# Expert weights of a layer's start in shorter runs and asked for earlier, with a longer search for addresses

## The chip, the core and the metric

The kernel runs on one core of a Trainium2 chip. The metric is the time of one execution on the device, in microseconds. TensorE (PE) multiplies matrices, VectorE (DVE), ScalarE (ACT) and GpSimd (POOL) do the work between, and SyncE (SP) issues transfers. Transfers from memory (HBM) into on-chip memory (SBUF) run on 16 DMA engines, which serve the queues of SP, ACT and POOL together. SBUF has 128 partitions; a transfer writes each partition's part as one or more contiguous runs.

## What is computed

Two layers over 512 latent tokens and 256 context tokens of width 1024, all in float32. Each layer mixes tokens in four branches, gates and merges them, multiplies by an output projection, adds the result to the residual, and then sends tokens through 16 experts chosen by the experts themselves. Cut to what matters here:

```python
x = x + gt1 * (merge(branches(h)) @ w_out)       # output projection and residual
h2 = modulate(rmsnorm(x), sh2, sc2)
aff = softmax(h2 @ w_router)                     # (tokens, 16)
g, idx = top_k(aff.T, 2 * N // 16)               # 64 of 512 latent, 32 of 256 context tokens each
xe = h2[idx]                                     # gathered rows
hid = silu(xe @ w_gate[e]) * (xe @ w_up[e])      # 1024 -> 1408
x = x + gt2 * scatter_add(idx, (hid @ w_down[e]) * g)
```

The last layer leaves the context tokens out after their keys and values. An expert's three matrices are 17.3 MB; all experts of both layers together are 554 MB.

## The kernel before

**Stages.** A layer is: projections, attention and gates (the mixers); `out_and_route`, which multiplies by the output projection in two halves of 512 columns, adds the residual, normalises, computes router affinities and the top-k, and stores the normalised rows `h` and intermediate `x_res` to buffers in HBM (`h2s`, for the context `h2c`) from which they can be gathered; `experts`, a loop over 16 experts. Layer 0 has three groups of gathered rows (two of latent tokens, one of context), layer 1 has two.

**Expert weights.** An expert has six blocks of 128 partitions by 5,632 floats (22,528 bytes a partition, 2.88 MB): two of gate and up weights for the first half of the contraction (A), two for the second (B), two of down weights (D). A block is one load with one run of 22,528 bytes per partition; a half block, one run of 11,264 bytes. All are issued on SP's queue by `ex_load` (lines 1403 for halves and 1397 for whole blocks) in the order of use. `queued` (from line 1380) keeps few in flight: a whole block's load waits until the load two before it has landed, a half's until the one two before a half; the first load after expert 0's gathers also waits for these gathers. SP issues in order, so whatever waits there holds what stands behind.

**The start of a layer's experts.** The first eight blocks are listed in `early` (line 1146): four halves of A and four of B of expert 0, then two whole blocks of expert 1's A and two of expert 0's D. `out_and_route` issues two of them behind the first residual, four after the loop of the second half of the projection; `tail`, called from `experts`, issues the rest (in layer 0 two are left until after the gathers). Eight whole blocks are as much as the arena holds.

**The arena.** Weights and the mixers' large tiles lie in one arena of 183,296 bytes per partition. The kernel is built twice: the first build gives each tile's life, from which `place` finds an address for each (first fit in order of birth, and a tile that finds none goes to the front of the order); the second build uses them. A tile that takes the place of an earlier one waits for that one's last reader.

**The stores and the gather.** `store_tokens` (line 1375) stores 128 rows as two DMAs of 64 rows of 4,096 bytes, on ACT's queue: per 128 latent tokens one pair to `xs` (in layer 1 to `out`), one to `h2s`. POOL's `gather` (line 1440) of expert 0 reads `h2s` by indices `idx` (line 1289), so it waits for all stores to `h2s`. DVE transposes the gathered rows to `xT` (line 1449), and PE multiplies (`gu_ps`, line 1467).

**Output projection weights.** `w_out` comes in six pieces of three or two row blocks, `wo_raws` (line 368, on SP), each cast by ACT and split by DVE into high and low parts (`wo_w`, lines 146 and 147). The gates' weights go the same way (`craw`, `cw`, 72 tiles). The residual's loads (`x_res`, lines 1367 and 1369) stand on SP's queue among them.

Of the kernel before, what the change touches and what calls it, by code (L numbers as in the profile page):

```python
# [19 lines left out]
D = 1024  # L20
# [3 lines left out]
L = 2  # L24
# [3 lines left out]
WB = 5632  # L28
QUEUED = 2
# [23 lines left out]
ARENA = 183296  # L53

# [12 lines left out]
def place(lives, room):  # L67


    order = sorted(range(len(lives)), key=lambda n: lives[n][0])  # L70
    for _ in range(1000):
        offs = {}
        for n in order:
            a, z, size = lives[n]
            near = [(offs[m], offs[m] + lives[m][2], *lives[m][:2]) for m in offs]
            busy = [(p, e) for p, e, f, t in near if f <= z and t >= a]
            best = None
            for o in sorted({0, room - size} | {e for _, e, _, _ in near} | {p - size for p, _, _, _ in near}):
                if o < 0 or o + size > room or any(o < e and p < o + size for p, e in busy):
                    continue  # L80
                key = max((t for p, e, f, t in near if t < a and p < o + size and o < e), default=-1), o
                if best is None or key < best:
                    best = key
            if best is None:
                break
            offs[n] = best[1]
        else:
            return [offs[n] for n in range(len(lives))]
        order.remove(n)
        order.insert(0, n)  # L90
    raise ValueError("no room")
# [6 lines left out]
class Block:  # L98
    def __init__(self, ctx, tc, io, out, plan=None):

        self.tc, self.nc, self.io, self.out, self.plan = tc, tc.nc, io, out, plan
        self.asked = []
# [334 lines left out]
    def stage1(self, l, extra=()):  # L437
        nc, io = self.nc, self.io
        last = l == L - 1
# [97 lines left out]
        self.proj("na", 0, lhs, qk, evac_qk(NA, ssn, 8, 64), fill=run([]), wait=6)  # L537
        self.proj("df", 1, lhs, qk, evac_qk(DF, ssd, 16, 32), fill=run(skewed(na_vec, na_tr)))
# [590 lines left out]
    def out_and_route(self, l, xs_src, x_dst, ctx_dst):  # L1129
        nc, io = self.nc, self.io  # L1130
        last = l == L - 1
# [15 lines left out]
        early += [lambda e=e, p=p: self.ex_load(l, e, p, 1) for e, p in ((1, "A"), (1, "A"), (0, "D"), (0, "D"))]  # L1147
# [164 lines left out]
        with self.tc.manual_schedule(engines=IN_ORDER):  # L1312
            stores = []
            resid(0, 0, acc.pop(order[0]))
            for _ in range(2):
                early.pop(0)()
# [28 lines left out]
            for _ in range(4):  # L1345
                early.pop(0)()
# [41 lines left out]
    def ex_load(self, l, e, part, n):  # L1388
# [3 lines left out]
        src = self.io["w_ex"][l, e]  # L1392
        b0 = 2 * "ABD".index(part)
        if n:
            t = self.Q([n, WB], "w_ex")
            at = b0 + (len(blocks) if part == "D" else len(blocks) // 2)
# [359 lines left out]
```

## Time and profile before

| | us |
| --- | --- |
| Median of three runs | 2761.74 (2754.11 to 2763.66) |
| Profiled execution, its own time | 2758.79 |
| Span of the profiled execution | 2756.7 |
| PE busy | 2423.7 (88%) |
| DVE, ACT, POOL busy | 991.1, 566.5, 454.9 |
| HBM read | 734 MB |

In the profile a row of the order of time gives start, length, engine, line, operation, `out<-in` and in brackets the idle time ahead of it with what ended it. SPq and ACTq are the queues on which SP and ACT issue transfers: a row there is the issue, not the transfer; rows in sequence are merged, with their count at the end, and the length then reaches from the first to the last. Tables by stretch give each engine's busy time within it, the granted TensorE clock as a share of full speed, the share of the DMA engines' time and what they moved.

### The profile page before, as it was taken

Reading aid. Unit: us, or ns where it says so; the run is one execution under the profiler, and the core shown is the slowest. Engines: PE = TensorE matmul, PEld = TensorE weight load, DVE = VectorE, ACT = ScalarE, POOL = GpSimd, SP = SyncE. Lnnn points to the kernel's source line nnn. Section 1 sums busy time; section 2 is a strip of 40 time slices with the busy share of each in tenths; the row PEclk is TensorE's granted clock in tenths of the full one; section 3 lists DMA queues with packets and bytes.
Section 4 is the critical chain, followed back from the end, with each engine's and each line's share of the span. In section 5 each row is a group of like instructions: output and inputs, shape, how many; then the busy total and the mean of one; then the engine's idle time right before and its main releaser. Section 6 shows DMA issues by size and latency. Waiting matters only on the chain. (4 is left out here: it accounts for less than half of the span.)

```text
span 2756.7 us, 48426 instructions
## 1 busy us (share of the span) xinstructions
PE 2423.7 (88%) x21318; PEld 1685.5 (61%) x21318; DVE 991.1 (36%) x1997; ACT 566.5 (21%) x1082; POOL 454.9 (17%) x335
## 2 busy tenths in 40 slices
PE   4889999999969999999998799999973977777776
PEld 3668988899844556777775577777861423222222
DVE  4975547553251111121112666477440110110100
ACT  4333334432310000000000434344320000000000
POOL 1532111121141111011101121011131110010100
PEclk9989999999979999999999899999986999999999
DMA  7574462431379999999998576544457999999998
GB/s 260 186 228 142 131 170 73 125 118 47 118 261 416 418 414 410 414 411 413 408 414 331 175 220 198 170 134 138 117 205 322 419 421 423 416 418 422 418 421 326
DMA packets 128177, 776.72 MB, mean 282 GB/s; under 512 B 13408, under 2 KB 51552, under 8 KB 101856
## 3 DMA queue, kind: packets, MB, share of 16 engines
q1 hardware_dynamic: 109888, 728.80, 67.8%
q0 software_dynamic: 11776, 25.44, 3.8%
q10 hardware_dynamic: 6304, 19.40, 2.4%
q8 instruction: 167, 2.74, 0.4%
q14 instruction: 42, 0.34, 0.0%
HBM read 734.01 MB, written 39.58 MB: 281 GB/s over the span
## 5 line engine op out<-in xcount | busy, mean ns | idle before, releaser
L1467 PE MATMUL gu_ps<-w_ex,xT 128*32 128x352 f32 x10240 | 819.4, 474 | 151.8 <-DMA w_ex<-in_w_ex 94.3
L1467 PEld LDWEIGHTS gu_ps<-w_ex,xT 128*32 128x32 f32 x10240 | 482.1, 113 | 484.3 <-issue 246.2
L577 PE MATMUL gate_ps<-hh,cw 128*128 128x384 f32 (+1 forms) x1536 | 451.8, 361 | 0.0
L1500 PE MATMUL dn_ps<-w_ex,hidT 128*32 128x512 f32 x2816 | 344.8, 596 | 38.3 <-DMA w_ex<-in_w_ex 36.4
L1476 ACT ACTIVATE hid<-gu_ps 128x352 f32<-128x352 f32 x80 | 37.1, 463 | 1290.4 <-PE gu_ps L1467 1290.4
L577 PEld LDWEIGHTS gate_ps<-hh,cw 128*128 128x128 f32 x1536 | 283.8, 190 | 27.9 <-issue 5.7
L577 PE MATMUL gate_ps<-hl,cw 128*128 128x384 f32 (+1 forms) x768 | 274.6, 358 | 0.0
L1500 PEld LDWEIGHTS dn_ps<-w_ex,hidT 128*32 128x32 f32 x2816 | 117.3, 110 | 231.9 <-issue 191.9
L1502 DVE SCALAR_TENSOR_TENSOR y_e<-dn_ps,gval,gt 128x512 f32<-128x512 f32 x32 | 24.0, 751 | 460.1 <-PE dn_ps L1500 460.1
L1477 DVE TENSOR_TENSOR hid<-hid,gu_ps 128x352 f32<-128x352 f32 x80 | 41.7, 521 | 363.8 <-ACT hid L1476 254.4
L577 PEld LDWEIGHTS gate_ps<-hl,cw 128*128 128x128 f32 x768 | 145.7, 190 | 9.1 <-issue 0.4
L147 DVE TENSOR_TENSOR cw<-craw,cw 128x1280 fp32r<-128x1280 f32 (+1 forms) x72 | 112.2, 1560 | 33.8 <-ACT cw L146 33.6
L991 POOL TENSOR_TENSOR acc<-acc,sg 128x384 f32<-128x384 f32 (+1 forms) x48 | 64.6, 1346 | 358.0 <-DVE sg L981 278.9
L1494 DVE SCALAR_TENSOR_TENSOR y_e<-dn_ps,gval,gt 128x256 f32<-128x256 f32 x16 | 7.7, 484 | 320.4 <-PE dn_ps L1492 320.4
L1481 POOL DMA_INDIRECT out<-y_e,idx x16 | 25.7, 1609 | 581.3 <-DVE y_e L1502 581.3
L1481 POOL DMA_INDIRECT cs<-y_e,idx x16 | 27.1, 1691 | 509.5 <-DVE y_e L1494 509.5
L255 DVE SCALAR_TENSOR_TENSOR ada_acc<-w_ada_k,scT,ada_acc 128x1024 f32<-128x1024 f32 x68 | 94.1, 1393 | 18.4 <-DMA w_ada_k<-in_w_ada 18.3
L1492 PE MATMUL dn_ps<-w_ex,hidT 128*32 128x256 f32 x1408 | 100.6, 379 | 0.0
L146 ACT CAST cw<-craw 128x1280 fp32r<-128x1280 f32 (+1 forms) x72 | 89.2, 1241 | 42.5 <-PE branch_ps L975 18.5
L971 ACT ACTIVATE sg<-gate_ps 128x384 f32<-128x384 f32 (+1 forms) x96 | 50.5, 526 | 187.3 <-PE gate_ps L577 175.1
L981 DVE SCALAR_TENSOR_TENSOR sg<-sg,branch_ps 128x384 f32<-128x384 f32 (+1 forms) x72 | 42.9, 596 | 112.6 <-PE branch_ps L975 105.3
L1492 PEld LDWEIGHTS dn_ps<-w_ex,hidT 128*32 128x32 f32 x1408 | 64.4, 110 | 22.9 <-issue 1.8
(342 smaller groups left out, 3194.6 us busy)
## 6 DMA issues: line engine op xcount, KB each, us to landing
w_ex<-in_w_ex SPq DMA_DIRECT2D x184, 2816.0 KB
w_ada_k<-in_w_ada SPq DMA_DIRECT2D x80, 512.0 KB
craw<-in_w_gb SPq DMA_DIRECT2D x64, 640.0 KB
w_ex<-in_w_ex SPq DMA_DIRECT2D x16, 1408.0 KB
qkv_raws<-in_w_qkv SPq DMA_DIRECT2D x12, 768.0 KB
w_ada<-in_w_ada SPq DMA_DIRECT2D x4, 1536.0 KB
wo_raws<-in_w_out SPq DMA_DIRECT2D x8, 768.0 KB
na_st<-qk_job SPq DMA_DIRECT2D x10, 512.0 KB
```

The lines of the kernel that those rows point to most:

```text
L146: self.nc.scalar.copy(hi, src)
L147: self.nc.vector.tensor_sub(lo, src, hi.bitcast(F32))
L255: nc.vector.scalar_tensor_tensor(a, t, sc, a, op0=OP.mult, op1=OP.add)
L577: nc.tensor.matmul(ps, w[:, lw, k], self.hT(lh, k, t0, t1), start=(k == 0 and s == 0), stop=(k == 7 and s == 2))
L971: nc.scalar.activation(sg, pg, AF.Tanh, scale=0.5)
L981: nc.vector.scalar_tensor_tensor(o, sg, 1.0, pb, op0=OP.add, op1=OP.mult)
L991: nc.gpsimd.tensor_add(ac, ac, sg)
L1467: nc.tensor.matmul(PG[e, g][s][32 * j:32 * j + 32], XT[e][:, g, c], self.w_gu(e, c, s, j), start=(c == 0), stop=(c == 7))
L1477: nc.vector.tensor_mul(t[:, g], t[:, g], pu)
L1481: nc.gpsimd.indirect_dma_start(out=x, out_offset=bass.IndirectOffsetOnAxis(ap=idx, axis=0), in_=y, in_offset=None, compute_op=OP.add)
L1492: nc.tensor.matmul(ps[32 * j:32 * j + 32], HT[e][:, 2, k], self.w_dn(e, k, 256 * j, 256 * j + 256), start=(k == 0), stop=(k == 10))
L1500: nc.tensor.matmul(ps[32 * q:32 * q + 32], HT[e][:, g, k], self.w_dn(e, k, 512 * h, 512 * h + 512), start=(k == 0), stop=(k == 10))
```

## The change

The first eight blocks of each layer lie in a new array `w_head` as 32 pieces of 128 by 1,408 floats, so that a whole block comes in four runs of 5,632 bytes per partition and a half in two; the destination in SBUF and the bytes are as before. `early` is issued earlier: right behind the residual's loads at the start of `out_and_route` two halves in layer 0 and five in layer 1, then two and one behind the first residual, four and two after the loop, the rest in `tail` as before. `place` is divided into three parts by two marks (the middle of layer 0's transition to the experts, and a point in layer 1's projections); within each it tries orders with a tile that found no room re-inserted at random, and lets whole and half blocks start at multiples of their size only.

```diff
+RUN = 1408
+HEAD = ((0, "A"), (0, "B"), (1, "A"), (0, "D"))
 QUEUED = 2
...
+SEEDS = 6, 1, 149
...
         early = [lambda p=p: self.ex_load(l, 0, p, 0) for p in "AAAABBBB"]
-        early += [lambda e=e, p=p: self.ex_load(l, e, p, 1) for e, p in ((1, "A"), (1, "A"), (0, "D"), (0, "D"))]
+        early += [lambda e=e, p=p: self.ex_load(l, e, p, 1) for e, p in HEAD[2:] for _ in range(2)]
+        for _ in range((2, 5)[l]):
+            early.pop(0)()
...
             resid(0, 0, acc.pop(order[0]))
-            for _ in range(2):
+            for _ in range((2, 1)[l]):
                 early.pop(0)()
...
             del self.aR, aR, ws
-            for _ in range(4):
+            for _ in range((4, 2)[l]):
                 early.pop(0)()
...
+        head = (e, part) in HEAD
+        t = self.Q([n, WB] if n else [WB // 2], "w_ex")
+        if head:
+            assert n < 2
+            r0 = int(4 * (2 * HEAD.index((e, part)) + done))
+            runs = 4 if n else 2
+            ins = self.nc.sync.dma_start((t[:, 0] if n else t).rearrange("p (r f) -> p r f", f=RUN),
+                                         self.io["w_head"][l, r0:r0 + runs].rearrange("r p f -> p r f"))
...
+def place_part(lives, room, part, seed, done, tries=150):
+
+    rnd = random.Random(seed)
+    order = sorted(part, key=lambda n: lives[n][0])
+    for _ in range(tries):
+        offs = dict(done)
         for n in order:
...
+            o = fit(lives, room, offs, n)
+            if o is None:
                 break
...
         order.remove(n)
-        order.insert(0, n)
-    raise ValueError("no room")
+        with_n = [i for i, m in enumerate(order) if m in offs and lives[m][0] <= lives[n][1] and lives[m][1] >= lives[n][0]]
+        order.insert(rnd.choice(with_n) if seed and with_n else 0, n)
```

On SP's queue, at the start of layer 1's output projection, before (`w_ex` are the expert weights' loads, the `128x2816` ones halves):

```order
L368 DMA wo_raws_15265<-in_w_out 128x2x512
L1403 DMA w_ex_15835<-in_w_ex 128x2816
L1367 DMA x_res_15615<-xs 64x1x1024 x6
L1367 DMA x_res_15616<-xs 64x1x1024 x2
L368 DMA wo_raws_15265<-in_w_out 128x3x512 x2
L1307 DMA pick<-in_pick 64x512
L1309 DMA pick_15826<-in_pick 64x256
L368 DMA wo_raws_15265<-in_w_out 128x2x512
L1403 DMA w_ex_15837<-in_w_ex 128x2816
L1403 DMA w_ex_16081<-in_w_ex 128x2816
```

and the same place after:

```order
L394 DMA wo_raws_15265<-in_w_out 128x2x512
L1429 DMA w_ex_15627<-in_w_head 128x2x1408
L1429 DMA w_ex_15631<-in_w_head 128x2x1408
L1397 DMA x_res_15615<-xs 64x1x1024 x6
L1397 DMA x_res_15616<-xs 64x1x1024 x2
L1429 DMA w_ex_15625<-in_w_head 128x2x1408
L394 DMA wo_raws_15265<-in_w_out 128x3x512
L1429 DMA w_ex_15629<-in_w_head 128x2x1408
L394 DMA wo_raws_15265<-in_w_out 128x3x512
L1429 DMA w_ex_15633<-in_w_head 128x2x1408
L394 DMA wo_raws_15265<-in_w_out 128x2x512
L1337 DMA pick<-in_pick 64x512
```

Five halves now stand around the residual's loads, three of them ahead of a piece of the output projection's weights each; before it was one, and none ahead of the last three pieces.

On PE, in layer 0, where the top-k's products stand among those of expert 0's context group, before (`gu_ps` are expert products, `top_ps` and `idx_ps` belong to the top-k of the latent tokens):

```order
L1467 MATMUL gu_ps_6646<-w_ex_6574,xT 32x352 x4
L1467 MATMUL gu_ps_6647<-w_ex_6574,xT 32x352 x4
L1275 MATMUL top_ps<-ident,topk 64x32 x2
L1281 MATMUL idx_ps<-topk,pick 128x32 x4
L1296 MATMUL idx_ps<-topk,pick_6149 128x32 x2
L1467 MATMUL gu_ps_6646<-w_ex_6576,xT 32x352 x4
```

and after:

```order
L1501 MATMUL gu_ps_6647<-w_ex_6574,xT 32x352 x4
L1501 MATMUL gu_ps_6646<-w_ex_6576,xT 32x352 x4
L1501 MATMUL gu_ps_6647<-w_ex_6576,xT 32x352
L1305 MATMUL top_ps<-ident,topk 64x32 x2
L1501 MATMUL gu_ps_6647<-w_ex_6576,xT 32x352 x3
L1501 MATMUL gu_ps_6646<-w_ex_6578,xT 32x352
L1311 MATMUL idx_ps<-topk,pick 128x32 x4
L1326 MATMUL idx_ps<-topk,pick_6153 128x32 x2
L1501 MATMUL gu_ps_6646<-w_ex_6578,xT 32x352 x3
```

The top-k's products have moved behind those of the next half (`w_ex_6576`), and part of the one after stands between them.

## Rows read from the trace of the kernel before

**Rows 1.** The page's slices of 69 us: the DMA engines' busy tenths.

```profile
DMA  7574462431379999999998576544457999999998
```

**Rows 2.** By stretch: length, busy us (instructions) per engine, PEclk, DMA share, GB/s.

```profile
20.00:40.00 20.00, 12.70 (x110) 9.07 (x110) 9.22 (x16) 7.59 (x13) 0.70 (x1) 1.00 1.03 390
180.00:690.00 510.00, 498.93 (x3076) 454.25 (x3077) 272.54 (x613) 195.99 (x407) 91.48 (x76) 0.99 0.41 125
830.00:1502.00 672.00, 670.42 (x8784) 447.63 (x8788) 106.19 (x170) 24.73 (x49) 86.00 (x69) 1.00 1.00 410
1510.00:1985.00 475.00, 434.09 (x2206) 345.35 (x2206) 303.21 (x616) 199.41 (x365) 82.76 (x62) 0.95 0.53 165
2104.00:2117.00 13.00, 7.50 (x72) 3.21 (x76) 1.27 (x2) 0.00 (x0) 7.74 (x8) 0.60 0.29 82
2200.00:2740.00 540.00, 412.41 (x4380) 155.81 (x4376) 57.23 (x89) 12.04 (x26) 40.33 (x33) 0.95 1.01 420
```

**Rows 3.** PE's waits from 2117 to 2740: us in total, times, longest.

```profile
PE gu_ps L1467 <- DMA w_ex<-in_w_ex: 91.1, 46, 3.3
```

**Rows 4.** PE in order of time, around both restarts: start, length, what.

```profile
830.23 10.18 PE L1467 MATMUL gu_ps<-w_ex,xT 128*32 128x352 f32 x108 [8.09 <-DVE xT L1449]
...
2065.83 1.04 PE L1296 MATMUL idx_ps<-topk,pick 64*128 64x32 f32 x4
2109.50 15.87 PE L1467 MATMUL gu_ps<-w_ex,xT 128*32 128x352 f32 x180 [42.63 <-DVE xT L1449]
```

**Rows 5.** POOL in order of time: the first gather of latent rows in each layer.

```profile
820.01 0.99 POOL L1440 DMA_INDIRECT xg<-h2s,idx  x1 [22.21 <-DMA w_ex<-in_w_ex]
...
2104.55 1.09 POOL L1440 DMA_INDIRECT xg<-h2s,idx  x1 [49.50 <-DMA h2s<-h]
```

**Rows 6.** DVE in order of time: the gather's indices in each layer.

```profile
811.33 0.25 DVE L1289 SCALAR_TENSOR_TENSOR idx<-topk,misc 128x32 int32<-128x32 f32 x1
...
2066.86 0.25 DVE L1289 SCALAR_TENSOR_TENSOR idx<-topk,misc 128x32 int32<-128x32 f32 x1
```

**Rows 7.** ACT's queue in order of time: issue of layer 1's last stores.

```profile
2059.85 4.05 ACTq L1375 DMA_DIRECT2D h2s<-h  x4
```

**Rows 8.** SP's queue in order of time, and its waits from 2030 to 2125.

```profile
690.07 2.58 SPq L1367 DMA_DIRECT2D x_res<-in_x  x4
...
722.95 85.42 SPq L1403 DMA_DIRECT2D w_ex<-in_w_ex  x8
...
2037.56 23.85 SPq L1403 DMA_DIRECT2D w_ex<-in_w_ex  x6
...
2116.85 0.33 SPq L1397 DMA_DIRECT2D w_ex<-in_w_ex  x1
...
SPq L1397 <- DMA xg<-h2s,idx: 20.4, 1, 20.4
...
SPq L1397 <- PE gu_ps L1467: 12.4, 2, 8.0
```

**Rows 9.** ACT's DMA queue in 808:820, 2040:2125, 2066:2104, 2075:2088: packets, MB, share.

```profile
q10 hardware_dynamic: 218, 0.78, 16.4%
...
q10 hardware_dynamic: 864, 3.15, 9.0%
...
q10 hardware_dynamic: 355, 1.29, 8.3%
...
q10 hardware_dynamic: 120, 0.43, 8.2%
```

**Rows 10.** ACT and PE in layer 1's output projection, in order of time.

```profile
2002.80 1.48 ACT L146 CAST wo_w<-wo_raws 128x1536 fp32r<-128x1536 f32 x1 [3.36 <-DMA wo_raws<-in_w_out]
...
2012.67 3.57 PE L1339 MATMUL wo_ps<-wo_w,acc_r 128*128 128x512 f32 x15
```

**Rows 11.** The page's groups of the gates' weights: split and cast, busy, mean ns.

```profile
L147 DVE TENSOR_TENSOR cw<-craw,cw 128x1280 fp32r<-128x1280 f32 (+1 forms) x72 | 112.2, 1560 | 33.8 <-ACT cw L146 33.6
...
L146 ACT CAST cw<-craw 128x1280 fp32r<-128x1280 f32 (+1 forms) x72 | 89.2, 1241 | 42.5 <-PE branch_ps L975 18.5
```

More of the change, by code (lines that the diff above doesn't have):

```diff
@@ L64, in lifetimes, with fit @@
     return [(*use[name], size) for name, size in asked]
[L67 to L72, printed above, removed]
-        for n in order:
[L74 to L84, printed above, removed]
+def fit(lives, room, offs, n):
+    a, z, size = lives[n]
+    near = [(offs[m], offs[m] + lives[m][2], *lives[m][:2]) for m in offs]
+    busy = [(p, e) for p, e, f, t in near if f <= z and t >= a]
+    some = {0, room - size} | {e for _, e, _, _ in near} | {p - size for p, _, _, _ in near}
+    best = None
+    for o in range(0, room - size + 1, size) if size in (4 * WB, 2 * WB) else sorted(some):
+        if o < 0 or o + size > room or any(o < e and p < o + size for p, e in busy):
+            continue
+        key = max((t for p, e, f, t in near if t < a and p < o + size and o < e), default=-1), o
+        if best is None or key < best:
+            best = key
+    return best and best[1]
@@ L91, in place @@
-    raise ValueError("no room")
+        with_n = [i for i, m in enumerate(order) if m in offs and lives[m][0] <= lives[n][1] and lives[m][1] >= lives[n][0]]
+        order.insert(rnd.choice(with_n) if seed and with_n else 0, n)
+def place(lives, room, marks):
+    done = {}
+    for z, (a, b) in enumerate(zip([0] + marks, marks + [len(lives)])):
+        for seed in (SEEDS[z], *range(40)):
+            offs = place_part(lives, room, range(a, b), seed, done)
+            if offs is not None:
+                break
+        else:
+            raise ValueError("no room")
+        done = offs
+    return [done[n] for n in range(len(lives))]
@@ L101, in __init__ @@
         self.tc, self.nc, self.io, self.out, self.plan = tc, tc.nc, io, out, plan
-        self.asked = []
+        self.asked, self.marks = [], []
         if plan is not None:
@@ L537, in stage1 @@
         self.proj("na", 0, lhs, qk, evac_qk(NA, ssn, 8, 64), fill=run([]), wait=6)
+        if last:
+            self.marks.append(len(self.asked))
         self.proj("df", 1, lhs, qk, evac_qk(DF, ssd, 16, 32), fill=run(skewed(na_vec, na_tr)))
@@ L1525, in experts @@
         gu(0, 0, 4, [0, 1])
+        if l == 0:
+            self.marks.append(len(self.asked))
         load(1, "B")
@@ L1737, in build @@
             if plan is None:
-                raise Planned(lifetimes(nc.m.functions[0].blocks[-1].instructions, b.asked))
+                raise Planned(lifetimes(nc.m.functions[0].blocks[-1].instructions, b.asked), b.marks)
     nc.finalize()
```

29 lines of the change are left out of this document (14 added, 15 removed).

## The prediction

> **What bounds the kernel now.** I read the 40 slices first: the DMA engines stand at 9 tenths in two blocks, slices 13 to 21 and 31 to 39, which are the expert loops [rows 1]. The table by stretch then says which of the two ends last where [rows 2]. In layer 0's loop (830 to 1502) PE is busy 670.42 of 672 us with the DMA engines full beside it: PE-bound, with the weights just ahead. In layer 1's loop from 2200 on PE is busy 412.41 of 540 us and the DMA engines are full at 420 GB/s: DMA-bound, and the longest of PE's waits from 2117 on is for `w_ex`, 91.1 us in the first products alone [rows 3]. The mixers are PE-bound: 498.93 of 510 us busy in layer 0, 434.09 of 475 in layer 1 [rows 2].
>
> Between mixers and loops lie the places this change is about. In layer 1 PE does nothing from 2066.9 to 2109.50 [rows 4], and from 2104 to 2117 the DMA engines, the resource that limits the rest of the layer, move 82 GB/s [rows 2]. The chain, followed back from PE's restart: expert 0's activations `xT` come from the gather `xg` at 2104.55; POOL had waited 49.50 us for the stores `h2s<-h` [rows 5], though the indices stood at 2067.1 [rows 6] and ACT's queue had issued the last store by 2063.9 [rows 7]. So the stores were on their way for 40 us. SP could not go on either: its next load waits for the gathers (20.4 us), then for PE to release a block (12.4 in two waits), and is issued at 2116.85 [rows 8]. Layer 0 has a smaller copy: indices at 811.6 [rows 6], gather at 820.01 after 22.21 us [rows 5] (the row names a `w_ex` landing, but the program has that gather wait for the stores and the indices alone), PE restart at 830.23 [rows 4].
>
> **Why the stores are slow.** The stores are rows of 4,096 B, 64 to a DMA. ACT's queue moved 768 of them (3.15 MB) from 2040 on; 315 (1.29 MB) were left at 2066 and took until 2104 [rows 9]. The pace depends on what runs beside them: 190 rows (0.78 MB) in the 12 us from 808, when most loads in flight were halves with runs of 11,264 B, that is 15.9 per us; 105 (0.43 MB) in the 13 us from 2075, beside whole blocks with runs of 22,528 B, that is 8.1 per us [rows 9]. Twice the run, half the pace: a store row seems to get its turn behind one run of the load. Runs of 5,632 B should then give between 15.9 (no further gain) and 31.8 (doubled once more); I take the harmonic middle, 21 per us, since the store row's own time doesn't shrink.
>
> **What the change does, part by part.**
>
> Runs of 5,632 B and early loads, layer 1. Moved: five halves are now asked for around the residual's loads and the sixth at the first residual, the last two halves after the loop, four whole blocks in the tail; before, two halves came early, a burst of six at 2037.56 [rows 8], and the whole blocks in the tail. That leaves about 2 halves and 4 blocks beside the stores instead of 6 and 4. At 21 rows per us, 546 rather than 453 rows are through in the 26 us to 2066, and the 222 left need 10.6 us: the gather starts near 2077 (with 0.4 for landing and start) instead of 2104.55. From gather to PE took 4.95 us with nearly idle DMA engines in layer 1 and 10.2 beside loads in flight in layer 0 [rows 4, 5]; with one short-run load beside it I take 6.65: PE at 2083.7, 25.8 us earlier. The next load then follows PE; by the order it waits one step of the contraction longer than before, and two block releases, each of two steps, lie 4.4 us apart (12.4 less the longest wait, 8.0) [rows 8], so 2.2 us are given back. As the rest of the layer is DMA-bound with the same bytes, the whole layer moves with that restart: **23.6 us**. Ends: gather straight behind the indices at 2068, PE at 2073, gives 34; a pace of only 15.9 gives 315 rows in 20 us, gather at 2087, gives 14.
>
> Layer 0. The last 190 rows need 9 us rather than 12, and 1.5 more go because the first two halves are asked for behind the residual's loads of 690 to 692.65, 30 us before 722.95 [rows 8]: gather at 815.5. The whole load behind the gathers is held back until they are done, so 6 us from there to PE: 821.5 instead of 830.23, **8.7 us**. The loop is PE-bound and shifts whole, provided that the weights come as much earlier: their stream restarts behind PE, so it does. Ends: 12.8 (gather right behind the indices, 4.95 to PE: 817.5) and 4 (gather unchanged in pace, only the latency better).
>
> Router order. `top_ps` and `idx_ps` of layer 0 now stand behind the sixth half's products, about 0.8 us later. Nothing, as the gather waits for stores until after that; 0.8 if it doesn't.
>
> More in front of the output projection's weights. In layer 1 the last three `wo_raws` loads now queue behind halves on SP, two of which wait for earlier halves. Before, the first of the three landed at 2002.8, where its cast of 1.48 us began; the split behind it takes some 1.9 (1.56 for 1,280 columns, here 1,536 [rows 11]), and PE first needs it at 2012.67 [rows 10]. That is 6 to 7 us of slack, against 3.4 for one half more in front and 6.9 for two (1.44 MB each at 420 GB/s). Nothing, or up to 6 us where it doesn't fit. In layer 0 the third's cast waits for PE and not for its load: nothing.
>
> Longer search for addresses. Other addresses mean other waits in the mixers. PE is idle there 11 us in layer 0 and 41 in layer 1 in all [rows 2], so little can be won; I put it at 0, with ±6.
>
> The load rate itself. Loads in runs of 4,096 and 6,144 B moved 390 GB/s in 20 to 40 us, against 410 to 420 in the loops [rows 2]: 46 MB cost at most 8 us more, all while PE has work or waits for the stores anyway. Nothing.
>
> Sum: 23.6 + 8.7 = 32.3 us. The profiled execution took 2758.8 us (span 2756.7); it becomes 2726.5. The runs' median, 2761.7, is 2.9 above it, which I leave in the range: **2726**.
>
> **A rule that speaks against it.** The Trainium skill, "DMA: Bandwidth & Descriptors", section "SWDGE vs HWDGE vs iDMA", gives a packet of preferably at most 4,096 bytes as the boundary at which a DMA engine turns to another queue. By that rule a run of 22,528 B would be left as often as one of 5,632 B, the run's length would change nothing, and 18 us of the sum would remain: 2741. The halving of the store pace between the two stretches above speaks against it, though they differ in more than the run. That is the second rival below.
>
> **The rivals.**
> - Stores quite out of the way: both gathers straight behind the indices. 34 + 12.8 = 46.8, 2712. For it: only two short-run loads may be in flight. Against: the eighth half and two blocks still run beside the last stores. 0.13.
> - The run's length does nothing, only the earlier loading counts: four halves (5.8 MB, 14 us at 420 GB/s) less run beside layer 1's stores, worth 14 us there, and 4 in layer 0, 2741. For it: the two paces come from stretches with different stores. 0.15.
> - The change doesn't do what it says: no room in the arena before the mixers' last tiles go, loads ahead wait, gathers stay where they are; ±6 from addresses: 2757. The order puts the loads' waits on a branch product near 1965 and on landings, which speaks against it. 0.06.
> - Slower: the new addresses make the mixers' weight splits wait for PE's last use of the tile just read. The place is `cw`, 72 tiles, a cast of 1.24 us and a split of 1.56 each [rows 11]; uncovered, a tile costs PE 2.8 us, all of them 202. It outweighs the 32 us from 12 tiles on and is slower by 0.3% from 15: 2767 to 2790, say 2772. Against: PE hardly waits for `cw` now, and the order leaves most tiles the distance they had. 0.05.
>
> **How the numbers follow.** Forecast 0.61 (2712 to 2741). Its own ends: 34 + 12.8 with 6 from addresses, 2706; 14 + 4 with 6 against, 2747. The range takes in the first two rivals: 2705 to 2746, leaving out the last two and the tails. About 0.3%, 8 us, is what a measurement can tell from no change; faster by more than that 0.87, within it 0.08, slower 0.05.
>
> **What would show it.** In the changed profile: POOL's first gather of layer 1 near 2077 with its wait on `h2s<-h` some 28 us shorter, PE's wait on `xT` near 17 instead of 42.6; ACT's queue moving about 21 rows per us beside short runs; the next load of SP near 2093; layer 0's PE restart near 821. The second rival would show the pace still at 8 to 16 and the gather near 2090. Wrong I am if PE shows new waits for `wo_w` or `cw`, or if the waits on `w_ex` in layer 1's loop grow by what the start gained.

## The result, and the profile after

The changed kernel takes 2745.05 us (median of four runs, 2740.41 to 2745.43) against 2759.86 for the kernel before on the same chip: a ratio of 0.994, 95% interval 0.9923 to 0.9956. A second set of nine runs on another chip gave 2745.97 against 2758.94, 0.9952 (0.9934 to 0.9969). So it is faster by 13 to 15 us, where 32 were forecast. The profiled execution took 2745.43 us with a span of 2743.7, 13.0 less than before.

The 40 slices still show the two full blocks of the expert loops; in the last one before layer 1's loop the DMA engines now stand at 8 instead of 7 tenths [rows 1].

```profile
DMA  7565452530669999999998666544468999999998
```

The same stretches of the trace after (columns as in [rows 2]) show both loops unchanged; the hole ahead of layer 1's loop has moved forward and is in part filled.

```profile
830.00:1502.00 672.00, 669.40 (x8756) 472.16 (x8760) 106.72 (x170) 24.78 (x49) 88.66 (x72) 1.00 1.00 409
2084.00:2103.00 19.00, 9.42 (x104) 4.05 (x108) 1.27 (x2) 0.00 (x0) 7.76 (x8) 0.64 0.69 257
2200.00:2740.00 540.00, 404.83 (x4324) 151.66 (x4313) 56.11 (x87) 12.08 (x26) 40.04 (x33) 0.96 0.99 410
```

PE in order of time after, around both restarts. They answer to 830.23 and 2109.50 in [rows 4]: layer 0's restart is 0.8 us later, layer 1's 15.9 us earlier.

```profile
831.05 4.33 PE L1501 MATMUL gu_ps<-w_ex,xT 128*32 128x352 f32 x32 [12.90 <-DVE xT L1483]
...
2093.58 6.88 PE L1501 MATMUL gu_ps<-w_ex,xT 128*32 128x352 f32 x61 [20.95 <-issue]
```

POOL after: the first gathers, 3.4 us later in layer 0 and 19.6 earlier in layer 1 [rows 5]. Both still wait for the stores.

```profile
823.40 0.99 POOL L1474 DMA_INDIRECT xg<-h2s,idx  x1 [21.32 <-DMA h2s<-h]
...
2084.95 1.09 POOL L1474 DMA_INDIRECT xg<-h2s,idx  x1 [23.96 <-DMA h2s<-h]
```

SP's queue after in layer 1 (start, length from first to last issue). The first load behind the gathers goes out at 2102.91 instead of 2116.85 [rows 8]; and two halves with a piece of `wo_raws` behind each are held until 2007 and 2013.

```profile
1989.80 0.39 SPq L1429 DMA_DIRECT2D w_ex<-in_w_head  x1
1990.29 0.41 SPq L394 DMA_DIRECT2D wo_raws<-in_w_out  x1
2007.24 0.37 SPq L1429 DMA_DIRECT2D w_ex<-in_w_head  x1
2007.70 0.42 SPq L394 DMA_DIRECT2D wo_raws<-in_w_out  x1
2013.01 0.37 SPq L1429 DMA_DIRECT2D w_ex<-in_w_head  x1
2013.48 0.41 SPq L394 DMA_DIRECT2D wo_raws<-in_w_out  x1
...
2102.91 24.68 SPq L1434 DMA_DIRECT2D w_ex<-in_w_ex  x5
```

ACT after shows the price: the casts of the last three pieces, the first of which stood at 2002.80 [rows 10] and the next two at 2005.18 and 2009.90.

```profile
2009.12 1.48 ACT L172 CAST wo_w<-wo_raws 128x1536 fp32r<-128x1536 f32 x1 [3.38 <-DMA wo_raws<-in_w_out]
...
2015.11 1.47 ACT L172 CAST wo_w<-wo_raws 128x1536 fp32r<-128x1536 f32 x1 [3.05 <-DMA wo_raws<-in_w_out]
...
2020.61 1.04 ACT L172 CAST wo_w<-wo_raws 128x1024 fp32r<-128x1024 f32 x1 [4.02 <-DMA wo_raws<-in_w_out]
```

**Where the 13.0 us come from.** I divide both profiled executions at PE's start on each output projection (its first `wo_sc` product), since the mixers ahead of them vary by some us from one execution to the next. A stage ends here where its last product starts: `wo_ps` for the projection, `gu_ps` for layer 0's loop. Layer 0 reaches its projection 3.8 us later; from there to the loop's last `gu_ps` product it takes 2.3 us less. From that product to layer 1's projection, mostly the mixers, it takes 1.0 us less. From the start of layer 1's projection to the end it takes 13.5 us less: the projection itself 5.2 more (58.9 to 64.1), from its end to the gather 25.3 less (60.9 to 35.6), from the gather to PE 3.7 more (4.9 to 8.6), from PE's restart to the end 2.9 more. 3.8 - 2.3 - 1.0 - 13.5 = -13.0.

**What the projection's 5.2 us are.** In the rows below, the stretch of the projection before and after and then a part of the latter (columns as in [rows 2]), PE is idle 2.4 us of it after and not at all before. 1.85 of that are two waits for `wo_w`, of 0.55 and 1.30 us, with one product between them. Right behind them, from 2019 to 2022.4, the granted clock is 0.51 of full speed, that is the lower of TensorE's two levels, 1.2 of 2.4 GHz; before it was 1.00 throughout. Four `x_tp` products take 1.11 us there instead of 0.60, and the 18 `wo_ps` behind them 5.30 instead of 4.36. Over the stage PE is busy 2.8 us longer for the same 324 products.

```profile
1984.70:2043.60 58.90, 58.90 (x324) 50.03 (x323) 20.87 (x43) 18.53 (x39) 15.00 (x11) 1.00 0.50 142
1985.20:2049.30 64.10, 61.73 (x324) 50.72 (x324) 21.10 (x43) 18.58 (x39) 15.84 (x11) 0.97 0.64 199
2019.00:2022.40 3.40, 3.40 (x11) 2.39 (x10) 1.29 (x2) 1.79 (x4) 2.51 (x2) 0.51 0.38 124
```

### The profile page after: what moved, and what is told of

Same layout as the page of the kernel before. It is cut to its first block, busy times and chain, and to the rows that moved or that the text cites. A ratio compares the mean times of both kernels' runs of the same rounds, so it can differ in the third digit from the quotient of the medians.

```text
span 2743.7 us, 48422 instructions
## 1 busy us (share of the span) xinstructions
PE 2428.5 (89%) x21318; PEld 1712.8 (62%) x21318; DVE 987.3 (36%) x1997; ACT 565.3 (21%) x1082; POOL 454.9 (17%) x335
## 5 line engine op out<-in xcount | busy, mean ns | idle before, releaser
L1501 PE MATMUL gu_ps<-w_ex,xT 128*32 128x352 f32 x10240 | 814.3, 471 | 134.2 <-DMA w_ex<-in_w_ex 93.5
L1501 PEld LDWEIGHTS gu_ps<-w_ex,xT 128*32 128x32 f32 x10240 | 497.3, 112 | 444.8 <-issue 223.2
L1534 PEld LDWEIGHTS dn_ps<-w_ex,hidT 128*32 128x32 f32 x2816 | 122.0, 110 | 229.7 <-issue 193.4
L1526 PEld LDWEIGHTS dn_ps<-w_ex,hidT 128*32 128x32 f32 x1408 | 65.9, 109 | 20.8 <-issue 1.5
```

What stands on the lines that cost most here:

```text
L1501: nc.tensor.matmul(PG[e, g][s][32 * j:32 * j + 32], XT[e][:, g, c], self.w_gu(e, c, s, j), start=(c == 0), stop=(c == 7))
L1526: nc.tensor.matmul(ps[32 * j:32 * j + 32], HT[e][:, 2, k], self.w_dn(e, k, 256 * j, 256 * j + 256), start=(k == 0), stop=(k == 10))
L1534: nc.tensor.matmul(ps[32 * q:32 * q + 32], HT[e][:, g, k], self.w_dn(e, k, 512 * h, 512 * h + 512), start=(k == 0), stop=(k == 10))
```

## The experiments

Where two kernels are compared, the stages above are used. Each row of the table is one profiled execution against that of before: layer 0 from its projection's start to the last `gu_ps` product of its loop, and from the start of layer 1's projection the four parts and their sum, in us. The last column is what SP's queue still had to move at 2190 us.

| kernel | layer 0 | projection | to gather | to PE | to end | sum | MB left |
| --- | --- | --- | --- | --- | --- | --- | --- |
| before | | | | | | | 224.14 |
| after | -2.3 | +5.2 | -25.3 | +3.7 | +2.9 | -13.5 | 218.82 |
| after_again | -2.3 | +6.2 | -25.4 | +4.0 | +1.4 | -13.8 | 217.02 |
| e1_long | +4.0 | +6.4 | -22.5 | +4.3 | +2.8 | -9.0 | 222.45 |
| e2_short | -3.0 | +0.6 | -22.1 | +3.8 | +6.7 | -11.0 | 218.26 |
| e3_332 | -4.5 | +9.2 | -25.7 | +3.8 | +2.9 | -9.8 | 222.74 |
| e4_704 | -7.5 | +7.6 | -26.1 | +2.8 | +2.4 | -13.3 | 214.61 |
| e5_pool | -3.4 | +8.8 | -25.4 | +3.2 | +3.2 | -10.2 | 220.85 |
| e5b_pool704 | -1.8 | +8.8 | -26.5 | +3.1 | +3.8 | -10.8 | 219.00 |
| e6_b704 | +3.1 | +0.1 | -30.1 | +3.9 | +16.3 | -9.8 | 221.30 |
| e7_p233_704 | -3.4 | +2.9 | -28.8 | +2.8 | +9.8 | -13.3 | 220.49 |
| e8_l0only | -3.9 | +1.6 | -26.2 | +3.4 | +16.0 | -5.2 | 219.45 |
| b1_defer | -7.7 | +6.4 | -31.0 | +4.1 | +3.4 | -17.1 | 215.01 |
| b1_again | -7.7 | +6.2 | -31.4 | +3.5 | +4.0 | -17.7 | 213.93 |
| b2_short_defer | -0.9 | +1.2 | -31.8 | +0.7 | +21.6 | -8.3 | 220.40 |
| b3_defer_loose | -6.1 | +4.1 | -30.7 | +4.6 | +2.6 | -19.4 | 216.25 |
| e10_loose | -1.2 | +4.3 | -25.1 | +3.2 | +2.7 | -14.9 | 217.20 |

**Order and addresses without short runs, and short runs alone.** e1_long keeps the changed kernel's order and search and takes the runs back; e2_short is the kernel before with the runs of 5,632 bytes and nothing else.

```diff
 # e1_long, against the changed kernel
-            ins = self.nc.sync.dma_start((t[:, 0] if n else t).rearrange("p (r f) -> p r f", f=RUN), ...
+            src = self.io["w_ex"][l, e, at]
+            ins = self.nc.sync.dma_start(t[:, 0] if n else t, src if n else src[:, h:h + WB // 2])
 # e2_short, against the kernel before: ex_load and w_head of the change
-            t = self.Q([n, WB], "w_ex")
+            ins = self.nc.sync.dma_start((t[:, 0] if n else t).rearrange("p (r f) -> p r f", f=RUN), ...
```

> The changed kernel with one run of 22,528 bytes (halves: 11,264) again for the first eight blocks; order, addresses and early issue stay as in the change. If the run's length sets the pace of the stores beside the loads (20.4 rows of 4,096 bytes per us in the changed kernel's layer 1), that pace falls to some 8 to 14 per us, the last store lands 15 to 25 us later, the first gather of layer 1 comes near 2100 to 2110 instead of 2085, and the time goes to 2757 to 2768. If only the earlier loading counts, the gather stays near 2085 and the time at 2745 within 4.

> The kernel before with runs of 5,632 bytes for the first eight blocks and nothing else: its own issue points, order and addresses. If the run's length sets the pace: 768 store rows at some 20 per us from 2040 on are through near 2079 instead of 2104, PE restarts near 2088 and the stream near 2096, 20 us earlier; nothing is lost in the mixers and the output projection, so the time is 2738 to 2744, at or below the changed kernel. If only the earlier loading counts: 2760, as before, gather of layer 1 still near 2104.

Against 2757.51 of the same chip, e1_long took 2753.66 (0.9984, 0.9974 to 0.9994) and e2_short 2744.24 (0.9952, 0.9935 to 0.9969). The runs alone give the whole gain, by the medians; the order and the addresses alone give 4 us. e2_short came out 0.2 us above what was expected, e1_long between its two theories: the pace of the stores fell as far as forecast, but the gather came at 2092.8, sooner than by the one theory (2100 to 2110) and later than by the other (2085). Layer 1's gather comes 22 us sooner after the projection in both, but for different causes: in e2_short because the stores pass, in e1_long because less is left to load beside them. From 2064 to 2076 ACT's queue there moved 95 rows by its bytes, 7.9 per us, where the changed kernel, which differs in the runs alone, moves 20.8 (below); from 2078 to 2082, with no load beside them, 50 per us.

```profile
q10 hardware_dynamic: 107, 0.39, 7.8%
```

In layer 0 the early order with long runs is a loss, its gather stands at 830.20:

```profile
830.20 0.99 POOL L1474 DMA_INDIRECT xg<-h2s,idx  x1 [29.20 <-DVE hid L1511]
```

**Shorter runs still.** e4_704 halves the runs of the changed kernel to 2,816 bytes, e6_b704 those of e2_short.

```diff
-RUN = 1408
+RUN = 704
```

> The changed kernel with runs of 2,816 bytes (704 floats) in the first eight blocks. If the run's length sets the pace: some 28 to 32 rows per us, stores through 8 to 12 us earlier, gather of layer 1 near 2074 to 2077 (then the indices, near 2073, are as late), time 2733 to 2739, unless such short runs lower the loads' own rate by more than the gain. If only the earlier loading counts: 2745.

> The kernel before with runs of 2,816 bytes in the first eight blocks, issue points as before. Theory A (the gather's date decides): stores at 28 rows per us are through near 2067 to 2070, PE restarts near 2076 to 2079, 10 us before the one with 5,632-byte runs, and the time falls by as much, to 2734 or so. Theory B (the bytes that the DMA engines have moved decide, since the rest of layer 1 is DMA-bound and they were busy without a hole there from 2037 on with 5,632-byte runs already): PE restarts earlier but waits for weights afterwards, the time stays at 2741 to 2745.

e4_704 took 2742.09 (0.9947, 0.9927 to 0.9968), above the 2733 to 2739 expected and not to be told from the changed kernel (0.9940 and 0.9952, with intervals that overlap this one); e6_b704 2748.58 against 2756.73 (0.9962, 0.9943 to 0.998), above both its theories. Now the pace can be read at three lengths. SP's and ACT's queues (packets, MB, share) in before from 2075 to 2088, where ACT's row is the last of [rows 9]; in after from 2068 to 2080; in e4_704 from 2044 to 2060:

```profile
q1 hardware_dynamic: 259, 5.11, 91.4%
```

```profile
q1 hardware_dynamic: 602, 3.30, 68.3%
q10 hardware_dynamic: 279, 1.02, 20.7%
```

```profile
q1 hardware_dynamic: 1437, 3.98, 64.1%
q10 hardware_dynamic: 509, 1.85, 30.9%
```

By bytes, since some packets are of a few bytes only, that is 105, 249 and 452 rows of 4,096: 8.1, 20.8 and 28.2 per us. Share times 16 engines times the stretch, over the count of runs or rows, is the time of one: a run takes 0.84, 0.22 and 0.12 us, a row 0.16, 0.16 and 0.18. Pace times (run and row) is 8.1, 8.0 and 8.2: at all three lengths it is as if eight engines took one run and one row in turn (several of each in turn would give the same pace). Which engines carry the rows the trace doesn't say; how many it does, by its landing events: each of these stores of 64 rows counts nine, one right behind the issue and eight as its rows land, and a load of weights sixteen. The Trainium skill, "DMA: Bandwidth & Descriptors", section "Why a DMA increments its semaphore by 16 and not by 1", has a transfer use the largest number of engines, up to 16, that divides the slowest dimension of both its sides; `store_tokens` writes 8 by 8 rows, which gives eight, and the product and the landings agree. e6_b704 shows the other half: the gather comes 8 us sooner after the projection than in e2_short, the program is not faster, since 16.3 us are lost behind PE's restart.

**Bytes, not the restart.** In the last column of the table lies the reason. Take e2_short: 218.26 MB at 0.42 MB per us (the rate of the loop, [rows 2]) are 519.7 us from 2190, and 32.7 more are its end at 2742.4. Worked out so, the rest is 31.8 to 33.3 us in all 17 profiled executions of this study, whatever the dates of gather and restart: layer 1's end is the number of bytes moved by a given date. The balance of SP's queue, by stretch (1960 to 2045, 2045 to 2085, 2085 to 2120, and, in the first two, from 2190 to the end), is first that of before, then after, then e2_short:

```profile
q1 hardware_dynamic: 2309, 9.49, 37.9%
...
q1 hardware_dynamic: 936, 12.31, 78.5%
...
q1 hardware_dynamic: 323, 6.38, 43.9%
...
q1 hardware_dynamic: 11197, 224.14, 92.4%
```

```profile
q1 hardware_dynamic: 3732, 13.68, 50.7%
...
q1 hardware_dynamic: 1982, 10.76, 69.5%
...
q1 hardware_dynamic: 987, 10.33, 72.2%
...
q1 hardware_dynamic: 10937, 218.82, 90.2%
```

```profile
q1 hardware_dynamic: 2892, 10.18, 40.6%
...
q1 hardware_dynamic: 2113, 11.36, 72.9%
...
q1 hardware_dynamic: 1448, 13.24, 93.7%
```

The changed kernel has 4.2 MB more through before 2045. But its eighth block, the last that the arena holds, is in at 2098, and the stream then stands until PE gives a block back: 10.3 MB at 72% in the third stretch, and 0.01 MB from 2098 to 2102. In e2_short the eighth block is still on its way in that stretch, hardly anything stands (13.2 MB at 94%), and the late start costs what the hole costs the other. That is why early issue on top of short runs brought so little.

**The early halves of layer 1.** e8_l0only is the changed kernel with layer 1's issue points of before; e3_332 asks for three halves at once and three at the first residual instead of five and one.

```diff
 # e8_l0only; e3_332 has (2, 3), (2, 3), (4, 2)
-        for _ in range((2, 5)[l]):
+        for _ in range((2, 0)[l]):
...
-            for _ in range((2, 1)[l]):
+            for _ in range((2, 2)[l]):
...
-            for _ in range((4, 2)[l]):
+            for _ in range((4, 4)[l]):
```

> The changed kernel with layer 1's early loads spread three, three, two, four instead of five, one, two, four, so that the last three pieces of the output projection's weights no longer wait behind halves that wait for other halves. If the 5.2 us that layer 1's output projection lost (its products lag the kernel before by 0.5 us at its start and 5.7 at its end) come from that queue: the lag goes, 3 to 5 us off, 2740 to 2742. If they come from other addresses: 2745, lag as in the changed kernel.

> The changed kernel with layer 1's eight halves issued where the kernel before issues them (none at the projection's start, two at the first residual, four after the loop, the rest in the tail); layer 0 as in the change, runs of 5,632 bytes. If the early halves cost layer 1's output projection its 5 us: the lag over the projection falls to under 1, the gather comes 39 us after the projection's end as in the kernel with short runs alone, and the time is 2743 to 2747, no worse than the change: then the early issue in layer 1 gives nothing. If the early issue gains more than it costs: 2749 to 2753.

e3_332 took 2750.75 against 2757.51 (0.9972, 0.9962 to 0.9982), e8_l0only 2748.48 against 2758.94 (0.9971, 0.9959 to 0.9984), with 2745.97 for the changed kernel on that chip. Without the early halves the projection's delay falls to 1.6 us, which speaks for them as its cause. It isn't a clean comparison: in e8_l0only the residual's loads also go out 6.6 us ahead of the projection, in the changed kernel 1.4 (below). By the medians the early halves are worth 2.5 us net, but the two intervals overlap, so that isn't shown. From layer 1's projection on they are worth 8 us in the table against e8_l0only, but only 2.5 against e2_short. The two differ although both have the issue points of before: e2_short's first half goes out 21 us ahead of the projection, as before, e8_l0only's at 2001.58, 23 us behind its start. For e3_332 I had expected the delay to shrink, as fewer halves stand ahead of the weights on SP: it grew to 9.2. That theory, of the order on SP alone, fell. Part of the growth is the clock, which over e3_332's projection has a mean of 0.95. Its time is longer for another reason too: between layer 0's loop and layer 1's projection its profiled execution took 7.4 us more than before, the changed kernel's 1.0 less; why isn't shown.

**What holds the projection's weights.** e5_pool moves the residual's loads of layer 1 to POOL's queue; e10_loose lets layer 1's first five halves wait for no landing, so that SP is not held.

```diff
 # e5_pool
-            self.load_tokens(rows_x[n], xs_src[0 if i < 4 else 1], i, (nc.sync, nc.sync))
+            self.load_tokens(rows_x[n], xs_src[0 if i < 4 else 1], i, ((nc.sync, nc.gpsimd)[l],) * 2)
 # e10_loose, in queued; self.loose is 5 in layer 1
-        for i in self.first + (self.big[-3:-2] if size < 1 else self.big[-QUEUED - 1:-QUEUED]):
+        free = self.loose > 0
+        self.loose -= 1
+        for i in self.first + ([] if free else self.big[-3:-2] if size < 1 else self.big[-QUEUED - 1:-QUEUED]):
```

> The changed kernel with layer 1's eight loads of the residual on POOL's queue instead of SP's; halves and output projection weights follow each other on SP as before. Theory: the 5.2 us lost in layer 1's output projection come from the queue, where the weights' last three pieces land behind the residual's rows (some 15 us of transfers on SP's queue) and the halves now between them. Then the pieces land 5 to 10 us earlier, the lag of PE over the output projection falls from 5.2 to under 1, and the time to 2739 to 2741. Rival, the DMA engines' total bandwidth in that stretch or other waits: lag 4 to 5 as before, 2745.

> The changed kernel, but layer 1's first five halves wait for no earlier load to land, so SP's queue is not held at the start of the output projection and the weights behind the halves are asked for at once; order, addresses and bytes are those of the changed kernel. Theory W (the output projection's delay of 5 to 6 us comes from halves that wait on SP for earlier halves' landings, and hold the weights behind them): the delay from the projection's start to its end falls under 3 us against the kernel before, and the time is 2741 to 2743. Theory T (it comes from the halves' transfers themselves, 1.44 MB each, which stand ahead of the weights in the DMA engines' queue whenever they are asked for): the delay stays at 5 to 7 us or grows, and the time is 2745 to 2747.

e5_pool took 2749.24 against 2756.73 (0.9972, 0.9959 to 0.9985) and missed: the delay was 8.8. e10_loose took 2746.51 against 2759.67 (0.995, 0.9933 to 0.9967). Its SP issues the fourth and fifth piece by 1990.5 (after: 1990.3 and 2007.7), and ACT's casts of them come 0.5 us later and 3.3 us sooner, with a projection that began 2.8 us sooner; the first fence is SP, the second ACT:

```profile
1986.98 0.90 SPq L1432 DMA_DIRECT2D w_ex<-in_w_head  x2
1988.57 1.90 SPq L394 DMA_DIRECT2D wo_raws<-in_w_out  x2
```

```profile
2009.62 1.48 ACT L172 CAST wo_w<-wo_raws 128x1536 fp32r<-128x1536 f32 x1 [0.48 <-DMA wo_raws<-in_w_out]
2011.80 1.47 ACT L172 CAST wo_w<-wo_raws 128x1536 fp32r<-128x1536 f32 x1 [0.69 <-DMA wo_raws<-in_w_out]
```

Ahead of the pieces in the queue stand the two halves of 1987 (2.8 MB) and the rest of the residual's rows of 4,096 bytes. SP's queue moves little there: from 1985 to 2010 4.77 MB after and 6.23 MB in e10_loose, that is 191 and 249 GB/s.

```profile
q1 hardware_dynamic: 1326, 4.77, 71.8%
```

```profile
q1 hardware_dynamic: 1873, 6.23, 85.0%
```

The delay is 4.3 us, between what the two theories gave (under 3, or 5 to 7), and the time is that of the changed kernel. So the weights come late also where SP is not held: from issue to cast the fourth piece takes 21.1 us, 18.8 after and 17.0 before. PE's idle time over the projection is no shorter (2.8 us, 2.4 after). What is gone is the lower clock: 1.00 on average over the projection here and in b3_defer_loose (below), 0.97 in the four executions with the changed kernel's order and waits (after, after_again, b1_defer, b1_again).

```profile
1982.40:2045.60 63.20, 60.37 (x324) 49.65 (x323) 21.09 (x43) 18.88 (x39) 17.36 (x11) 1.00 0.58 178
```

Not all of the delay need be the halves. The residual's loads, on which the pieces wait in SP's order, go out 4.1 us ahead of the projection before and 1.4 after, and 1.4 in e10_loose too; SP waits there for a `gate_ps` product of PE (17.2 us before, 5.8 after), as a tile does that takes the place of an earlier one. The rows are before, then after. e3_332, with 3.9 us and the longest delay, speaks for the halves; how the changed kernel's delay divides between the two no run separates.

```profile
1980.61 5.07 SPq L1367 DMA_DIRECT2D x_res<-xs  x8
```

```profile
1983.85 5.85 SPq L1397 DMA_DIRECT2D x_res<-xs  x8
```

**Two more of both kinds.** e7_p233_704 is e4_704 with two halves at once, three at the first residual and three after the loop; e5b_pool704 is e4_704 with e5_pool's edit.

```diff
 # e7_p233_704, against e4_704
-        for _ in range((2, 5)[l]):
+        for _ in range((2, 2)[l]):
...
-            for _ in range((2, 1)[l]):
+            for _ in range((2, 3)[l]):
...
-            for _ in range((4, 2)[l]):
+            for _ in range((4, 3)[l]):
```

> The changed kernel with runs of 2,816 bytes and layer 1's early loads spread two, three, three, four, so that only one half stands between the residual's loads and the output projection's weights. If halves ahead of those weights cost the output projection its 5 to 8 us, the lag falls to under 3 and the time to 2736 to 2739, against 2742 for 2,816-byte runs with the changed kernel's issue points; if not, 2742 to 2746.

> Both together: runs of 2,816 bytes and layer 1's residual loads on POOL's queue. If the two effects add: 2742 less 5 to 7 is 2735 to 2737. If the output projection's lag has another cause: 2742.

2750.27 (0.9974, 0.9961 to 0.9987) and 2744.81 (0.9956, 0.9941 to 0.9971) against 2756.73: neither beats e4_704. The first has the delay down to 2.9 and the gather 3.5 us nearer the projection than after, and gives it back behind the restart (+9.8): bytes again. Its sum there, -13.3, is e4_704's; what it lacks against e4_704 lies in layer 0 (-3.4 for -7.5) and between the layers, where its profiled execution took 5.0 us more than before and e4_704's 2.8 less. As in e3_332, why isn't shown.

**The same kernel again.**

> The changed kernel once more, for the spread of its mixers. Its first profile lagged the kernel before by 3.8 us at layer 0's output projection. If that comes from the new addresses and order, it is there again within 0.5 us. If it is the spread of single executions, it comes out anywhere between -1 and 4. Time 2743 to 2747 either way.

2745.97 (2733.20 to 2750.96): one kernel's executions lie up to 18 us apart. Here layer 0 reaches its projection 0.1 us sooner than before, not 3.8 later, so that delay was the execution's and not the addresses'; the projection's delay in layer 1 (6.2) and the gather came again.

**Fewer stores ahead of the gather.** The gather waits for the stores to `h2s` only, and the last two tiles' residual stores, to `xs` or `out`, stand among them on ACT's queue. b1_defer puts these behind, in both layers of the changed kernel; b2_short_defer does it in e2_short.

```diff
-        xTs = {}
+        xTs, late = {}, []
...
-                self.store_tokens(x_dst if i < 4 else ctx_dst, rows_x[n], i, nc.scalar)
+                f = lambda: self.store_tokens(x_dst if i < 4 else ctx_dst, rows_x[n], i, nc.scalar)
+                late.append(f) if n >= N - 2 else f()
...
-            for f in stores:
+            for f in stores + late:
```

> The changed kernel with the stores of the last two tiles' residual (256 rows of 4,096 bytes to the output, or to the next layer's input) put behind the stores that the gather reads, in both layers. If the gather waits for nothing but rows in ACT's queue at 20.4 per us: 12.5 us fewer before it, so the gather of layer 1 starts right behind the indices, 10 to 12 us earlier, that of layer 0 6 to 8 us earlier; the stream restarts 10 us earlier, some of it with a block still to land: 2728 to 2736. If the loads' bytes or other waits hold it: no earlier than 2741.

> The same putting back of stores on the kernel before with runs of 5,632 bytes alone. Its stream had no hole at the restart, but 1.6 MB still to land there, so an earlier gather can give less: 2736 to 2742. It is 2730 or under only if the date of the gather and not the bytes decides.

> The changed kernel with the deferral alone, a second time, beside the other two. Both theories: 2733 to 2738, that is 21 to 25 us under the kernel before; if the 22 us of its first look were an execution's chance, 2742 to 2746 as the changed kernel.

> The changed kernel with the last two tiles' residual stores put behind those to the gather's buffer, and layer 1's first five halves waiting for no landing. By theory W the projection ends 3 us sooner, the gather and the stream of weights with it: 2731 to 2733. By theory T nothing is won over the deferral alone: 2735 to 2737.

b1_defer took 2735.27 against 2758.94 (0.9918, 0.9894 to 0.9941) and, again, 2736.57 against 2759.67 (0.9913, 0.9896 to 0.993): 23 us under the kernel before, about ten under the changed one. b2_short_defer took 2747.21 (0.9961, 0.9947 to 0.9974), no better than e2_short and above the 2736 to 2742 expected. b3_defer_loose, with e10_loose's edit on top, took 2736.14 (0.9902, 0.988 to 0.9923): the same as without, as the theory of the transfers had it. In b1_defer POOL's gather stands at 2075.05 and the balance of SP's queue (the first three stretches) reads:

```profile
2075.05 1.09 POOL L1475 DMA_INDIRECT xg<-h2s,idx  x1 [17.68 <-DMA h2s<-h]
```

```profile
q1 hardware_dynamic: 3702, 14.45, 55.1%
...
q1 hardware_dynamic: 1714, 9.34, 61.3%
...
q1 hardware_dynamic: 1197, 14.15, 97.2%
```

Of the 9.0 us by which b1_defer beats the changed kernel in the table, 5.4 lie in layer 0, which is PE-bound and shifts with its gather, and 3.6 in layer 1 (b1_again: 5.4 and 4.2). In layer 1 the early halves and an early gather pay together: with the early halves alone the stream stands in the third stretch (after), with the early gather alone too few bytes are in (b2_short_defer), and here it has 14.45 MB early and 97% in the third.

## Why the prediction was right or wrong

The time lies in its range and the sign is right; the gain is under half of the 32.3 us, and each part can be set beside its term. That the range holds the time says little for the mechanism: 2745 is nearest to the 2741 of the rival by which the run's length does nothing, and that rival is false.

- **What bounds the kernel: right.** Layer 0's loop from PE's restart to its last product took 662.4 us before and 663.1 after, so it shifts whole. Layer 1 is DMA-bound. The stores were the chain: gather and PE's restart moved with them.
- **The pace: right, the number in part by luck.** 21 rows per us were forecast beside short runs, 20.8 measured. But the 15.9 from which 21 was worked out averages a stretch with gaps in the loads (under layer 0 below); beside runs of 11,264 bytes the kernel before moved 0.34 MB of rows from 2062 to 2068, 13.8 per us, and the same harmonic middle from there is 18.4. The rival that the run's length does nothing falls: the changed kernel and e1_long differ in the run alone, and so do e2_short and the kernel before. The rule cited from the Trainium skill ("DMA: Bandwidth & Descriptors", section "SWDGE vs HWDGE vs iDMA"), of packets of preferably at most 4,096 bytes as the boundary, would have 8.1 rows per us at every length; 8.1, 20.8 and 28.2 were measured, so the turn follows the run here, and the measurement decides. The page gives that row among the descriptors that GpSimd builds, and these loads and stores are issued by SP and ACT, which the prediction passed over.
- **From the gather to the next load: nearly right.** Gather to PE 8.6 us instead of 6.65; the next load 9.3 behind PE (2093.58 to 2102.91), 9.55 forecast.
- **"Nothing, or up to 6 us where it doesn't fit": a failed step, the wrong end taken.** I set 6 to 7 us of slack against 3.4 us for one half in front and 6.9 for two, and took the term as nothing. The three casts came 6.3, 9.9 and 10.7 us later. Of the first's 6.3, 3.2 are the residual's loads, which go out that much later (1983.85 for 1980.61; 0.5 of it is the projection's own date) and stand in no term; what remains is about the one half as priced. The second piece was asked for 17 us behind the first (before, 2), since SP was held. The projection took 5.2 us longer, and with it indices, stores and gather; more than half of that is not PE's waiting but products that took longer, in good part at a granted clock of 0.51 (above), which no term has either. SP's queue moves 191 GB/s there, not 420, but before it moved no more, 3.98 MB in the same 25 us, so the rate alone isn't the error. That the halves cause the rest is supported by e3_332 and e8_l0only, but no run changes them alone.
- **The gather at 2077.** It came at 2084.95. Of the 8 us, 5.7 are the projection's end, which I counted at its old date (5.2 and 0.5 from the mixers), the rest the stores.
- **Layer 0, 8.7 us: wrong, 2.3.** The other failed step is "The last 190 rows need 9 us rather than 12, and 1.5 more go because the first two halves are asked for behind the residual's loads". SP's and ACT's queues from 804 to 812, before and then after:

```profile
q1 hardware_dynamic: 118, 1.19, 40.5%
q10 hardware_dynamic: 333, 1.20, 37.6%
```

```profile
q1 hardware_dynamic: 333, 1.79, 60.6%
q10 hardware_dynamic: 185, 0.68, 20.9%
```

  Before, the loads left gaps there and 293 rows passed in 8 us, 37 per us; after, loads run all along and rows pass at 21. I had taken one average pace, 15.9, for a stretch that holds a free part and a full one. Nor does issuing early win 1.5: by e1_long, where it stands without short runs, layer 0 loses 4.0 us. What is left of the gain is mostly that from gather to PE, 10.2 to 7.7 us.
- **"The whole layer moves with that restart": right here, not in general.** Where PE restarts late the stream stands and waits for it (after: 2.9 us given back, 2.2 forecast). Where the eight blocks aren't in yet, an earlier restart is worth nothing (e6_b704, b2_short_defer). The currency is bytes.
- **Addresses and load rate, 0 each: not refuted in the mixers.** e2_short has the old search and the whole gain, and between the layers the changed kernel took 1.0 and 1.9 us less in two executions; waits for `cw` of a size to matter did not come. Waits for `wo_w` did, 1.85 us in the projection, and the residual's later loads there may be the addresses' (above). In layer 1's loop the waits on `w_ex` hardly grew, 93.5 us for 91.1 [rows 3]:

```profile
PE gu_ps L1501 <- DMA w_ex<-in_w_ex: 93.5, 48, 3.7
```

In sum: layer 1's 23.6 became 13.5 (5.2 by the projection, 2.2 by the gather's distance from it, 2.0 by the way to PE, 0.7 behind it), layer 0's 8.7 became 2.3, and 2.8 us of this execution lie in the mixers.

## What to carry to other kernels

Where small stores must pass beside bulk loads, give the loads short runs for that time: what a row waits for is the run ahead of it. In a stretch bound by transfers keep a balance in bytes moved by a date, not in dates of restarts: loading earlier and restarting earlier each pay only as far as the other keeps the stream from standing. And what is asked for early stands ahead of everything asked for later, so a load that the next stage needs at once goes first, or the early bytes are taken back from it. What a short wait costs is read from the rows behind it too: here 1.85 us of waiting came with 3.4 us at half the clock.

## What the runs showed that I had not expected

- The pace of 4,096-byte rows beside loads follows one line at run lengths from 2,816 to 22,528 bytes: rows per us times the time of one run and one row is 8.0 to 8.2.
- Runs of 2,816 bytes cost load rate. From 2085 to 2120 SP's queue moved 13.55 MB at 97.6% in e6_b704, and 14.37 MB at 98.8% in e8_l0only; by share that is 397 against 416 GB/s, and both stretches end with loads in runs of 22,528, so the short runs themselves differ by rather more. The first fence is e6_b704, the second e8_l0only.

```profile
q1 hardware_dynamic: 3581, 13.55, 97.6%
```

```profile
q1 hardware_dynamic: 1821, 14.37, 98.8%
```

- A store's issue can be held by a load: in the changed kernel the four issues of `h2s<-h` reach from 2056.14 over 16.49 us, where before they took 4.05 [rows 7]; by the trace's semaphore events the last pair went out when a load of expert weights landed. The rows ahead were still on their way then, so it cost nothing here.

```profile
2056.14 16.49 ACTq L1405 DMA_DIRECT2D h2s<-h  x4
```
